# A mixer's state-space scan and gated network: context outputs and context network placed beneath the scan, one block of modulation products moved into the gated network, read-out tables and Toeplitz blocks in one array

## The chip, the cores and the metric

The kernel runs on one core of a Trainium2 chip. The metric is the device time of one execution in microseconds (us), the median of several runs. All times below are in microseconds unless they are marked otherwise.

## The reference, cut to what matters

The program is a small transformer block stack over 1024 latent positions and 256 context positions with 1024 channels (eight tiles of 128 channels each). The part that the change touches is the mixer of layer 0: a bidirectional state-space layer (S5), a pointwise GELU, a gated network, and a projection. Cut down, with names as in the program:

```
u   = modulate(norm(x)) @ w_s5_in                 # [1024 channels, 1024 latent + 256 context]
X_t = A X_{t-1} + B u_t                           # complex states, forward and backward, 64 groups
z   = gelu(C X + Toeplitz(P) u)                   # read-out tables times states, plus a local part
y   = (z @ w_s5_glu[u-half]) * sigmoid(z @ w_s5_glu[g-half])
x  += gate * (y @ w_s5_out)
mods[l, b] = silu(c) @ w_mod[l, b] + b_mod        # 24 blocks, two layers of 12, needed by later parts
```

Time is cut into chunks of 8 positions, so a state is stored for 128 latent chunks and 32 context chunks, and each of the 64 groups of 16 channels has three 128 by 128 blocks for the outputs: two read-out tables (real and imaginary part of C times powers of A) and one Toeplitz block (the part of the output within a chunk).

## The kernel before

The program is one long stream per engine: TensorE (PE) for products, VectorE (DVE) for the scan and the sums, ScalarE (ACT) for copies out of PSUM and activations, GpSimd (POOL) for a few products and stores, SyncE (SP) for nearly all loads. The order on each engine is fixed when the program is built; a wait of one instruction holds all that stand behind it on its engine. DMAs that SP or ACT issues share a small set of completion semaphores in rotation, so that a DMA also waits for one that was issued eight before it.

The parts around the change, in order of time:

- **Input projection** (0 to about 164): w_s5_in times the modulated input. DVE and POOL build tables beside it; read-out tables go to the DRAM array dT (`to`, L405), the Toeplitz part P goes to dPF (L436, L437), the projected input goes to dUL (latent) and dUC (context).
- **State input** (about 160 to 240): sixteen units, two for each block `fb` of eight groups. `s5_u_load` (L454 to L458) brings one block's input U into SBUF (one latent load, two copies of the context part), DVE builds the unit's table (L476), PE transposes it (L502), ACT copies it (`tin`, L504), PE multiplies (`s5_in`, L515, L516), and ACT writes the result into the state array X (L518). Units 0 to 7 fill X of the groups 0 to 31, units 8 to 15 that of the groups 32 to 63.
- **Scan** on DVE: `sa` over groups 0 to 31, `sb` over groups 32 to 63 (L537, L541, L543; three operations make one step). In its first 32 steps a scan carries latent and context states together (operations of double width), after that latent alone. Beneath it, PE runs the modulation products: 20 blocks here, each loaded by SP in eight pieces of 256 KB (`gw`, L164), multiplied (L174, columns of four quarters of the array at once), copied by ACT (L177), transposed (L184) and added to `mods` (L195, L196).
- **S5 outputs**, one block fb after the other: SP loads U again (L454, L455), the tables `tt` (L565 or L571) and the eight pieces of the Toeplitz block `G` (L574); ACT or DVE copies the states (`S`, L585 to L589); PE multiplies 24 products of 161 columns (L601, L603: 128 latent, one empty, 32 context); ACT applies GELU (L604); POOL stores dZL and dZC (L605, L606).
- **Gated network** on w_s5_glu: SP loads dZL back (16 loads) and dZC (8 loads), L1621; then, for each of the eight tiles, seven Winograd products of the latent part (`ffn_step`, L978, 12 records of 512 columns each for one half) and two products `G` and `U` of the context part (L988, 24 records of 256 columns each). Weights `wr` come by SP (L906), ACT and DVE round and sum them (L936, L940).
- Then the projection w_s5_out (L121 to L125), attention and the feed-forward networks, which the change leaves as they are.

Of the kernel before, what the change touches and what calls it, by code (L numbers as in the profile page):

```python
# [6 lines left out]
F32 = mybir.dt.float32  # L7
# [6 lines left out]
P = 128  # L14
# [14 lines left out]
class Kernel:  # L29
# [170 lines left out]

    def mod(self, l, w):

        return self.mods[:, l, 8 * w:8 * w + 8, :]
# [6 lines left out]
class S5(Kernel):  # L210
# [8 lines left out]
    def s5_load(self):  # L219
# [3 lines left out]
        self.CN = po.tile([P, NG, 2, 16], F32, name="CN")  # L223
# [6 lines left out]
    def s5_params(self):  # L230
# [126 lines left out]
        self.PO = self.prmo.tile([P, 3, 8, NG], F32, name="PO")  # L357
# [37 lines left out]
    def s5_out_table(self, u):  # L395
# [9 lines left out]
        nc.gpsimd.dma_start(self.dT[u // 2, :, 4 * (u % 2):4 * (u % 2) + 4], t[:, :, :, 1:9, :])  # L405
# [32 lines left out]


# [7 lines left out]
    def s5_u_load(self, pool, fb, both, bufs=3):  # L447
# [4 lines left out]
        uc = self.dUC[fb].rearrange("(p g) c -> p g c", g=8)  # L452
        nc.scalar.activation(U[:, :, 161:162], self.zero, AF.Copy)
        nc.sync.dma_start(U[:, :, 33:161], ul)  # L454
        nc.sync.dma_start(U[:, :, 162:194], uc)  # L455
        if both:
            nc.scalar.activation(U[:, :, 32:33], self.zero, AF.Copy)
            nc.sync.dma_start(U[:, :, 0:32], uc)  # L458
        return U

# [35 lines left out]
    def s5_in_trans(self, t):  # L496
        nc = self.nc
        tin = self.inpool.tile([P, 8, P], F32, tag="tin", bufs=3, name=self.nm("tin"))
# [59 lines left out]
    def s5_out_load(self, fb):  # L558
        nc = self.nc
        g0 = 8 * fb  # L560
        U = self.s5_u_load(self.upool, fb, False, 4)
        src = self.dT[fb].rearrange("p g r q c -> p g r (q c)")
        if fb % 4 < 2:
            t = self.upool.tile([P, 8, 2, 128], F32, tag="tt", bufs=2, name=self.nm("tt"))
            nc.sync.dma_start(t, src)  # L565
            tt = [t[:, 2 * i:2 * i + 2] for i in range(4)]
        else:

            tt = [self.gpool.tile([P, 2, 2, 128], F32, tag="gw", name=self.nm("tt")) for _ in range(4)]
            for i in range(4):  # L570
                nc.sync.dma_start(tt[i], src[:, 2 * i:2 * i + 2])  # L571
# [4 lines left out]
        return U, tt, G  # L576

    def s5_states(self, fb, vector):
# [4 lines left out]
        S = self.upool.tile([P, 8, 2, 161], F32, tag="S", bufs=2, name=self.nm("S"))  # L583
        if vector:
            nc.vector.tensor_copy(S[0:64], X[0:64, gs, :, 0:161])  # L585
        else:
            nc.scalar.activation(S[0:64], X[0:64, gs, :, 0:161], AF.Copy)
        nc.scalar.activation(S[64:128, :, :, 0:128], X[64:128, gs, :, 127::-1], AF.Copy)
        nc.scalar.activation(S[64:128, :, :, 128:161], X[64:128, gs, :, 161:128:-1], AF.Copy)  # L589
        return S  # L590

    def s5_out(self, fb, loaded, S):

        nc = self.nc
        U, tt, G = loaded
        Z = self.upool.tile([P, 8, 161], F32, tag="Z", bufs=2, name=self.nm("Z"))
        for a, n in ((0, 3), (3, 3), (6, 2)):
            ps = self.psum()
            for k in range(n):
                o = ps[:, 161 * k:161 * k + 161]  # L600
                nc.tensor.matmul(o, G[:, a + k, :], U[:, a + k, 33:194], start=True, stop=False)  # L601
                for ri in range(2):
                    nc.tensor.matmul(o, tt[(a + k) // 2][:, (a + k) % 2, ri, :], S[:, a + k, ri, :], start=False, stop=(ri == 1))  # L603
# [1480 lines left out]
```

## Time and profile before

| what | value |
|---|---|
| time, median of 3 runs | 3369.47 (3367.6 to 3373.42) |
| the profiled execution: its own time, and span of its instructions | 3376.47, 3372.8 |
| PE busy in the span | 3196.8 (95%) |
| DVE busy | 2057.7 (61%) |
| ACT busy | 1383.7 (41%) |
| POOL busy | 266.7 (8%) |
| data moved | 375.67 MB, mean 111 GB/s |

PE is the busiest engine over the whole span, but not in every stage: the shares are means over stages with different limits. The profiled execution is 7.0 us above the median of the timed runs. "PEclk" in the profile is the clock of TensorE that was granted, in shares of the full 2.4 GHz; a value between 0.5 and 1 in a window means that part of it ran at the lower level of 1.2 GHz.

### The profile page before, as it was taken

The page shows a single profiled execution, that of the slowest core. Times are in us where ns is not written, and L with a number is a line of the kernel's source. Part 1 is how long each engine was busy: PE and PEld are TensorE (multiplying, and loading weights), DVE is VectorE, ACT ScalarE, POOL GpSimd, SP SyncE. Part 2 cuts the span into 40 slices and gives each one's busy share as a digit, 9 for nine tenths or more (in the row PEclk, how much of TensorE's full clock was granted, in tenths as well). Part 3 has the DMA queues.
Part 4 walks back from the last instruction along what each step waited for, and adds up shares of the span by engine and source line. Part 5 has one row for each costly group of instructions (what it writes and reads, how often), then busy time and mean ns, then how long its engine had stood idle before and what let it go on. Part 6 is the DMA issues. An engine that isn't in the chain of part 4 may idle for free.

```text
span 3372.8 us, 47213 instructions
## 1 busy us (share of the span) xinstructions
PE 3196.8 (95%) x17814; PEld 2692.5 (80%) x17814; DVE 2057.7 (61%) x4313; ACT 1383.7 (41%) x2708; POOL 266.7 (8%) x286
## 2 busy tenths in 40 slices
PE   8999669998899999999999999999889999999997
PEld 5763558886788888888878899999778888888787
DVE  7789737545764444523666888886557445444645
ACT  3351434235432222412553577774453223233433
POOL 1230100010000000000012310001100000000000
PEclk9999879998899999999999999999989999999998
DMA  7679962241231122524521100002223221235534
GB/s 254 170 208 322 249 175 88 94 156 63 84 101 68 69 68 71 187 88 131 161 85 58 62 23 17 21 15 76 81 80 104 71 72 65 72 125 173 177 124 145
DMA packets 227668, 375.67 MB, mean 111 GB/s; under 512 B 54432, under 2 KB 111040, under 8 KB 226672
## 3 DMA queue, kind: packets, MB, share of 16 engines
q1 hardware_dynamic: 206416, 326.73, 30.5%
q0 software_dynamic: 7632, 25.35, 2.5%
q10 hardware_dynamic: 13392, 20.58, 1.7%
q8 instruction: 139, 2.28, 0.3%
q14 instruction: 89, 0.73, 0.1%
HBM read 291.84 MB, written 80.74 MB: 110 GB/s over the span
## 4 chain that ended last, share of the span: by engine, by line
PE 81%; DVE 12%; DMA 3%; ACT 2%; issue 1%; SPq 1%; ACTq 0%; POOL 0%; DVEq 0%; POOLq 0%
PE ps L978 28%; PE ps L121 10%; PE ps L123 10%; PE ps L125 10%; PE ps L988 8%; PE ps L1425 2%; DVE sw L537 1%; PE ps L1445 1%; PE ps L1446 1%; PE ps L1444 1%; PE ps L1383 1%; PE ps L1384 1%; PE ps L1385 1%; DVE X L543 1%; DVE sw L541 1%
## 5 line engine op out<-in xcount | busy, mean ns | idle before, releaser
L978 PE MATMUL ps<-pg,pg 128*128 128x512 f32 x4368 | 1035.8, 395 | 39.1 <-ACT pg L936 22.8
L978 PEld LDWEIGHTS ps<-pg,pg 128*128 128x128 f32 x4368 | 823.9, 191 | 217.0 <-ACT pg L936 24.6
L121 PE MATMUL ps<-pg,pg 128*128 128x512 f32 (+1 forms) x1872 | 635.2, 363 | 19.5 <-ACT pg L102 8.0
L125 PE MATMUL ps<-pg,pg 128*128 128x512 f32 (+1 forms) x1872 | 626.9, 358 | 4.8 <-DVE pg L103 4.8
L123 PE MATMUL ps<-pg,pg 128*128 128x512 f32 (+1 forms) x1872 | 629.7, 359 | 0.3
L121 PEld LDWEIGHTS ps<-pg,pg 128*128 128x128 f32 x1872 | 348.2, 191 | 81.4 <-ACT pg L102 9.7
L125 PEld LDWEIGHTS ps<-pg,pg 128*128 128x128 f32 x1872 | 348.2, 191 | 60.3 <-DVE pg L103 8.0
L123 PEld LDWEIGHTS ps<-pg,pg 128*128 128x128 f32 x1872 | 348.7, 191 | 55.1 <-DVE pg L132 1.7
L988 PEld LDWEIGHTS ps<-pg,pg 128*128 128x128 f32 x2496 | 320.9, 195 | 24.3 <-DVE pg L940 10.0
L988 PE MATMUL ps<-pg,pg 128*128 128x256 f32 x2496 | 326.3, 287 | 13.9 <-DVE pg L940 8.7
L103 DVE TENSOR_TENSOR pg<-wr,pg 128x512 fp32r<-128x512 f32 (+1 forms) x312 | 219.5, 733 | 189.5 <-ACT pg L102 115.2
L102 ACT ACTIVATE pg<-wr 128x512 fp32r<-128x512 f32 (+1 forms) x312 | 175.4, 596 | 271.2 <-DMA wr<-in_w_ffn_out 89.2
L940 DVE TENSOR_TENSOR pg<-pg,pg 128x512 fp32r<-128x512 f32 x208 | 142.5, 688 | 136.3 <-ACT pg L936 129.2
L940 DVE TENSOR_TENSOR pg<-wr,pg 128x512 fp32r<-128x512 f32 x232 | 158.1, 687 | 104.4 <-ACT pg L936 102.5
L936 ACT ACTIVATE pg<-pg 128x512 fp32r<-128x512 f32 x208 | 127.2, 628 | 154.5 <-DVE pg L931 59.0
L132 DVE TENSOR_TENSOR pg<-ps,pg 128x512 fp32r<-128x512 f32 (+1 forms) x210 | 141.9, 676 | 57.8 <-ACT pg L131 52.5
L936 ACT ACTIVATE pg<-wr 128x512 fp32r<-128x512 f32 x232 | 139.5, 624 | 79.6 <-PE ps L988 37.2
L1405 ACT ACTIVATE pg<-ps,nb,rq 128x512 f32<-128x512 f32 x192 | 148.9, 777 | 5.4 <-DVE sm L1414 2.4
L131 ACT ACTIVATE pg<-ps 128x512 fp32r<-128x512 f32 (+1 forms) x210 | 123.9, 591 | 64.1 <-PE ps L1425 47.6
L1155 POOL TENSOR_TENSOR pg<-pg,pg 128x512 f32<-128x512 f32 x8 | 10.7, 1332 | 1763.5 <-DVE pg L631 864.5
L631 DVE SCALAR_TENSOR_TENSOR pg<-ps,mods,pg 128x512 f32<-128x512 f32 x64 | 47.9, 749 | 165.4 <-PE ps L125 160.7
L1390 DVE TENSOR_REDUCE mx<-ps 128x1 f32<-128x512 f32 (+1 forms) x208 | 137.1, 661 | 1.3 <-PE ps L1385 1.3
(339 smaller groups left out, 4450.6 us busy)
## 6 DMA issues: line engine op xcount, KB each, us to landing
wr<-in_w_ffn_in SPq DMA_DIRECT2D x104, 512.0 KB, 3.5
gw<-in_w_mod SPq DMA_DIRECT2D x192, 256.0 KB, 5.2
wr<-in_w_ffn_out SPq DMA_DIRECT2D x80, 512.0 KB, 3.9
dI<-pg SPq DMA_DIRECT2D x104, 256.0 KB, 2.0
pg<-dI SPq DMA_DIRECT2D x104, 256.0 KB, 4.6
wr<-in_w_ffn_out SPq DMA_DIRECT2D x40, 384.0 KB, 4.0
dX<-pg ACTq DMA_DIRECT2D x48, 256.0 KB, 2.0
pg<-dX SPq DMA_DIRECT2D x48, 256.0 KB, 4.2
```

Of the source, the lines that this page charges most:

```text
L102: nc.scalar.activation(hi, x, AF.Copy)
L103: nc.vector.tensor_tensor(lo, x, hi.bitcast(F32), op=ALU.subtract)
L121: mm(ps[c], wh, rh[c], start=first, stop=False)
L123: mm(ps[c], wh, rl[c], start=False, stop=False)
L125: mm(ps[c], wl, rh[c], start=False, stop=last)
L132: self.nc.vector.tensor_tensor(lo, src, hi.bitcast(F32), op=ALU.subtract)
L936: nc.scalar.activation(hi, self.isum[i, name], AF.Copy)
L940: v.tensor_tensor(lo, self.isum[i, name], hi.bitcast(F32), op=ALU.subtract)
L978: mm(e[bank], p[:, o], q, start=(first and k == 0 and j == 0), stop=(k == 3 and j == 2), skip_group_check=True)
L988: mm(ps, p[:, o], q, start=(k == 0 and j == 0), stop=(k == KT - 1 and j == 2))
L1390: v.tensor_reduce(mx[:, kc:kc + 1], ps, axis=AX.X, op=ALU.max)
L1405: nc.scalar.activation(p, u["bank"].pop((qt, kc)), AF.Exp, bias=nb[:, 0:1], scale=rq, accum_out=sm[:, kc:kc + 1])
```

## The change

It has three parts.

1. **Layer 1's modulation** (12 of the 20 blocks that ran beneath the scan) becomes 48 quarter blocks in the gated network. `gemv_next` (new) multiplies one quarter that is there and loads the next but two, four loads of 128 KB each on ACT's DMA queue; after each fourth quarter come one copy and four transposes. It is called for each unit of the network's start from the third on, and once in each later step.
2. **The context's outputs and its whole gated network** become items of a list (`ctx_items`, new) that are run beneath the scan, at the places where the clock of the program's builder passes their time. They use PE (32 columns for the outputs, 256 for the network, without Winograd sums), ACT (copies, GELU, sigmoid) and POOL (stores, loads of dZC, products). The latent outputs shrink from 161 to 128 columns, the gated network that follows is started without a context part, and the eight dZC loads ahead of it are gone.
3. **Tables and Toeplitz blocks lie in one DRAM array dW**: the tables are stored into it by POOL in pieces of 512 B, the Toeplitz part is spread into it by eight DMAs from DRAM to DRAM (`s5_shifts`, 512 KB each) that SP issues when unit 5 starts, and an output block then needs one load of 1.5 MB instead of `tt` and eight pieces of `G`. The context input is loaded once into SBUF (`Uc`), and ACT copies it twice into each block's U (`s5_u_fill`, ahead of the copies of unit 2fb-1).

```diff
+    def gemv_next(self):
+        nc = self.nc
+        if len(self.gv) == 3 or not self.todo and self.gv:
+            l, b, z, t = self.gv.pop(0)
+            if z == 0:
+                self.gp = self.psum()
+            h, a = z // 2, z % 2
+            for q in range(4):
+                nc.tensor.matmul(self.gp[32 * q:32 * q + 32, 256 * h:256 * h + 256], self.sS[:, 4 * a + q, :], t[q],
+                                 start=(a == 0), stop=(a == 1), tile_position=(0, 32 * q), skip_group_check=True)
+            if z == 3:
+                s = self.page()
+                nc.scalar.activation(s, self.gp, AF.Copy)
+                self.gemv_fin(l, b, self.gemv_tr(s))
+        if self.todo:
+            l, b, z = self.todo.pop(0)
+            t = [self.half() for _ in range(4)]
+            for q in range(4):
+                nc.scalar.dma_start(t[q], self.I["w_mod"][l, b, :, 4 * (z % 2) + q, 256 * (z // 2):256 * (z // 2) + 256])
+            self.gv.append((l, b, z, t))
...
+    def s5_shifts(self):
+        src = self.dPF.rearrange("g c t h -> c g (t h)")
+        for i in range(8):
+            self.nc.sync.dma_start(self.dW[16 * i:16 * i + 16].rearrange("p f g r c -> p (f g) r c")[:, :, 2],
+                              src[:, :, 16 * (7 - i):16 * (7 - i) + 128])
...
+    def s5_u_fill(self, fb, U):
+        for o in (32, 161):
+            self.nc.scalar.activation(U[:, :, o:o + 1], self.zero, AF.Copy)
+        for o in (0, 162):
+            self.nc.scalar.activation(U[:, :, o:o + 32], self.Uc[:, 8 * fb:8 * fb + 8, :], AF.Copy)
...
-        G = self.upool.tile([P, 8, 128], F32, tag="G", bufs=4, name=self.nm("G"))
-        for i in range(8):
-            nc.sync.dma_start(G[16 * i:16 * i + 16],
-                              self.dPF[g0:g0 + 8].rearrange("g c t h -> c g (t h)")[:, :, 16 * (7 - i):16 * (7 - i) + 128])
...
+    def ctx_items(self):
...
+        def out(fb, h):
+            U, t = ld[fb]
...
+            for k in range(4 * h, 4 * h + 4):
+                o = ps[:, 32 * k:32 * k + 32]
+                nc.tensor.matmul(o, t[:, k, 2, :], U[k], start=True, stop=False)
+                for ri in range(2):
+                    nc.tensor.matmul(o, t[:, k, ri, :], sc[fb][:, k, ri, :], start=False, stop=(ri == 1))
...
+        def net(t, h, ks=range(KT)):
...
+            for k in ks:
+                nc.tensor.matmul(ps, W[2 * t + h][:, P * k:P * k + P], self.zc[:, k, :], start=(k == 0), stop=(k == KT - 1))
...
+                nc.gpsimd.tensor_tensor(u, u, sc["g"], op=ALU.mult)
+                nc.gpsimd.dma_start(self.dI[t][:, 1024:1280], u)
...
         self.x_start(zz)
-        for c in (0, 1, 2):
+        for c in (0, 1):
             zload(c)
...
+                for _ in range(GN if k > GK else 0):
+                    self.gemv_next()
...
         def one(u):
+            if u == 0:
+                self.s5_u_fill(0, U[0])
+            if u % 2 and u < 15:
+                self.s5_u_fill(u // 2 + 1, U[u // 2 + 1])
             self.nin += 1
+            if self.nin == 6:
+                self.s5_shifts()
             self.s5_in(u, tin.pop(u), U[u // 2])
             if u % 2 and u // 2 + 2 < 8:
-                U.append(self.s5_u_load(self.inpool, u // 2 + 2, True, 2))
+                U.append(self.s5_u_load(self.inpool, u // 2 + 2, 2))
```

**SP's queue at the state input.** These are the issues on SP before, from the input of block 2 (U_1865) to that of block 5 (U_2162):

```order
L454 DMA U_1865<-dUL 128x8x128
L455 DMA U_1865<-dUC 128x8x32
L458 DMA U_1865<-dUC 128x8x32
L454 DMA U_1967<-dUL 128x8x128
L455 DMA U_1967<-dUC 128x8x32
L458 DMA U_1967<-dUC 128x8x32
L454 DMA U_2071<-dUL 128x8x128
L455 DMA U_2071<-dUC 128x8x32
L458 DMA U_2071<-dUC 128x8x32
L454 DMA U_2162<-dUL 128x8x128
```

And now, over the same four blocks (U_2103 is block 4):

```order
L484 DMA Uc<-dUC 128x256
L485 DMA U_1887<-dUL 128x8x128
L484 DMA Uc<-dUC 128x256
L485 DMA U_1990<-dUL 128x8x128
L467 DMA dW<-dPF 1024x1x128 x8
L484 DMA Uc<-dUC 128x256
L485 DMA U_2103<-dUL 128x8x128
L484 DMA Uc<-dUC 128x256
L485 DMA U_2195<-dUL 128x8x128
```

The eight copies from DRAM to DRAM stand between the loads of block 3 and block 4.

**ACT's queue at units 6 and 7.** Before, the tables (`tin`) and the copies into X (X_1697 is the array of groups 0 to 31) follow each other; these are the last rows of unit 6 and the first of unit 7:

```order
L518 ACTIVATE X_1697<-ps_2113 128x2x161
L518 ACTIVATE X_1697<-ps_2119 128x2x161
L504 ACTIVATE tin_2125<-ps_2126 128x512
L504 ACTIVATE tin_2125<-ps_2132 128x512
L518 ACTIVATE X_1697<-ps_2138 128x2x161
```

Now, at the same place (the array is X_1711):

```order
L551 ACTIVATE X_1711<-ps_2142 128x2x161
L551 ACTIVATE X_1711<-ps_2148 128x2x161
L537 ACTIVATE tin_2154<-ps_2155 128x512
L537 ACTIVATE tin_2154<-ps_2161 128x512
L490 ACTIVATE U_2103<-zero 128x8 x2
L492 ACTIVATE U_2103<-Uc 128x8x32 x2
L551 ACTIVATE X_1711<-ps_2171 128x2x161
```

The fill of block 4's U, which waits for that block's load, stands ahead of unit 7's copies into X.

**PE in the gated network.** Before, a context product `U` (L988) stands between the latent products of two tiles:

```order
L988 MATMUL ps_5212<-pg_5193,pg_5099 128x256 x2
L988 MATMUL ps_5212<-pg_5193,pg_5107 128x256
L978 MATMUL ps_5109<-pg_5067,pg_5105 128x512
L978 MATMUL ps_5109<-pg_5065,pg_5139 128x512
L978 MATMUL ps_5109<-pg_5089,pg_5105 128x512
```

Now, in the network's start, quarter blocks (L210; `hp` are the half pages into which ACT's queue loads w_mod) and transposes (L184) stand between the products (L1100):

```order
L1100 MATMUL ps_5074<-pg_4733,pg_4936 128x512
L210 MATMUL ps_4962<-hp_4967,sS 32x256
L210 MATMUL ps_4962<-hp_4968,sS 32x256
L210 MATMUL ps_4962<-hp_4969,sS 32x256
L210 MATMUL ps_4962<-hp_4970,sS 32x256
L1100 MATMUL ps_4987<-pg_4737,pg_4851 128x512
```

The context products are gone from there, and each step has four short products of another shape.

## Rows read from the trace of the kernel before

**Rows 1.** Windows: PE, PEld, DVE, ACT, POOL busy (count), PEclk, DMA share, GB/s.
```profile
250.00:300.00 50.00, 48.23 (x190) 15.48 (x188) 49.79 (x202) 5.32 (x16) 2.16 (x8) 0.99 0.95 320
...
450.00:500.00 50.00, 27.70 (x100) 21.25 (x101) 23.10 (x37) 20.47 (x35) 1.73 (x2) 0.76 0.64 167
...
600.00:680.00 80.00, 80.00 (x428) 69.37 (x428) 38.70 (x65) 24.82 (x47) 0.00 (x0) 1.00 0.27 93
```

**Rows 2.** Timeline of SP: start, duration, queue, line, transfer.
```profile
180.33 1.18 SPq L454 DMA_DIRECT2D U<-dUL  x1
...
189.56 0.52 SPq L454 DMA_DIRECT2D U<-dUL  x1
```

**Rows 3.** Timeline of ACT, then DVE, at the scan's start.
```profile
195.34 2.08 ACT L518 ACTIVATE X<-ps 128x322 f32<-128x322 f32 x4
...
197.52 0.73 DVE L537 TENSOR_TENSOR sw<-X,sm 128x256 f32<-128x256 f32 x1 [1.94 <-ACT X L518]
```

**Rows 4.** DMA issues: count, KB each, median us to landing.
```profile
U<-dUL SPq DMA_DIRECT2D x16, 512.0 KB, 5.0
```

**Rows 5.** Chain that ended last, 400 to 500: start, us, what.
```profile
405.09 9.24 DMA G<-dPF
...
449.47 0.45 ACT Z L604
...
450.52 5.93 DMA dZL<-Z
...
463.34 0.83 SPq L1621
...
471.27 4.46 DMA wr<-in_w_s_glu
```

**Rows 6.** Timeline of DVE: the first step that is single-width in both scans.
```profile
301.08 0.26 DVE L541 TENSOR_TENSOR sw<-sw,X 128x64 f32<-128x64 f32 x1
```

**Rows 7.** Timeline of PE: modulation blocks, then outputs.
```profile
264.25 1.05 PE L184 MATMUL ps<-sel,gs 128*128 128x2 f32 x8
...
270.48 1.05 PE L184 MATMUL ps<-sel,gs 128*128 128x2 f32 x8
...
371.02 1.41 PE L603 MATMUL ps<-S,tt 128*128 128x161 f32 x4 [11.45 <-DVE S L585]
...
376.36 0.43 PE L601 MATMUL ps<-U,G 128*128 128x161 f32 x2
...
377.18 0.43 PE L601 MATMUL ps<-U,G 128*128 128x161 f32 x2
```

**Rows 8.** Line L184: counts, durations in ns, first and last start.
```profile
L184 PE MATMUL ps<-sel,gs x192: 169/251/353, 13.0 to 351.2; 128*128 128x2 f32 x192
```

**Rows 9.** Timeline of PE: context product, half a modulation block; PEld: weight loads of one.
```profile
557.68 3.04 PE L988 MATMUL ps<-pg,pg 128*128 128x256 f32 x24
560.55 5.63 PE L978 MATMUL ps<-pg,pg 128*128 128x512 f32 x24
...
14.01 1.06 PE L174 MATMUL ps<-gw,sS 128*32 128x512 f32 x8
...
265.24 0.23 PEld L174 LDWEIGHTS ps<-gw,sS 128*32 128x32 f32 x4
```

**Rows 10.** Timeline of DVE and POOL at 700; POOL's groups by line.
```profile
700.12 4.01 DVE L103 TENSOR_TENSOR pg<-wr,pg 128x512 fp32r<-128x512 f32 x4
699.96 1.28 POOL L1155 TENSOR_TENSOR pg<-pg,pg 128x512 f32<-128x512 f32 x1 [247.71 <-DMA wr<-in_w_s_out]
701.19 1.20 POOL L1155 TENSOR_TENSOR hp<-hp,hp 128x256 f32<-128x256 f32 x1
...
L1157 POOL TENSOR_TENSOR hp<-hp,hp 128x256 f32<-128x256 f32 x20 | 18.4, 920 | 43.4 <-DVE hp L631 43.4
```

**Rows 11.** DVE's costliest group of that shape on its own.
```profile
L940 DVE TENSOR_TENSOR pg<-pg,pg 128x512 fp32r<-128x512 f32 x208 | 142.5, 688 | 136.3 <-ACT pg L936 129.2
```

**Rows 12.** Line L1582, issues on ACT's queue: ns minimum, median, maximum.
```profile
L1582 ACTq DMA_DIRECT2D dX<-pg x48: 326/326/849, 780.9 to 2499.9; - x48
```

More of the change, by code (lines that the diff above doesn't have):

```diff
@@ L594, in s5_out @@
         nc = self.nc
-        U, tt, G = loaded
-        Z = self.upool.tile([P, 8, 161], F32, tag="Z", bufs=2, name=self.nm("Z"))
-        for a, n in ((0, 3), (3, 3), (6, 2)):
+        U, t = loaded
+        Z = self.upool.tile([P, 8, 128], F32, tag="Z", bufs=2, name=self.nm("Z"))
+        for a in (0, 4):
             ps = self.psum()
-            for k in range(n):
-                o = ps[:, 161 * k:161 * k + 161]
-                nc.tensor.matmul(o, G[:, a + k, :], U[:, a + k, 33:194], start=True, stop=False)
+            for k in range(a, a + 4):
+                o = ps[:, 128 * (k - a):128 * (k - a) + 128]
+                nc.tensor.matmul(o, t[:, k, 2, :], U[k], start=True, stop=False)
@@ L602, in s5_out @@
                 for ri in range(2):
[L603 to L606 removed]
+                    nc.tensor.matmul(o, t[:, k, ri, :], S[:, k, ri, :], start=False, stop=(ri == 1))
@@ L886, in x_rest, with i_start @@
         self.x_flush()
-    def i_start(self, win, pairs, first):
+    def i_start(self, win, pairs, first, ctx=True):
         self.win = win
@@ L1063, in ffn_body @@
                     self.x_all(*{"P6": ("T3",), "P5": ("T4",), "P7": ("B22",)}.get(kind, ()))
+                for _ in range(GN):
+                    self.gemv_next()
         self.X = self.hs = self.xr = self.xt = self.ev = None
@@ L1889, in mixer0 @@
         todo = [(0, b) for b in range(4, 12)] + [(1, b) for b in range(12)]
+        NGV = len(todo) - GL
         g, sm, tp = [self.gemv_load(*todo[0])], {}, {}
         gk = [0]
+        self.todo, self.gv = [(l, b, z) for l, b in todo[NGV:] for z in range(4)], []
         def gemv_step():
@@ L1940, in mixer0, with counted @@
         self.prm.release()
+        self.upool = tc.alloc_tile_pool(name="uo", bufs=2, side="left", reuse_waits="tile")
+        def counted(gen):
+            for k, t in enumerate(gen):
+                if k == 3 * 33:
+                    items.append(self.ctx_items())
+                yield t
+        sb = counted(sb)
+        self.ld = []
         drive(sa, sb, 1)
-        while gk[0] < 20:
+        while gk[0] < NGV + 2:
             gemv_step()
-        self.upool = tc.alloc_tile_pool(name="uo", bufs=2, side="left", reuse_waits="tile")
-        ld = [self.s5_out_load(i) for i in range(4)]
         self.dense = False
@@ L1975, in mixer0 @@
             clock(10)
-        while gk[0] < 22:
-            gemv_step()
+        for it in items:
+            for _, f in it:
+                f()
         self.upool.release()
+        self.prmo.release()
         self.gpool.release()
```

193 lines of the change are left out of this document (132 added, 61 removed).

## The prediction

> **What bounds the kernel now.** I read the busy time by windows first. While the scan runs, DVE has no gap (49.79 of 50 us between 250 and 300); at the end of the output stage no engine is full (PE 27.70 of 50 between 450 and 500, its granted clock 0.76); in the gated network PE is full (80.00 of 80) [rows 1]. So the stretch has three limits, and a part of the change is worth what it does to the limit of its own stage. Then the chain of waits, for the stage in which nothing is full: it goes through loads of Toeplitz pieces (9.24 us for the block that starts at 405), the last GELU at 449.47, the store of dZL (5.93), the sixteen loads of dZL, the eight of dZC (463.34 to 471.27), and the weight load behind them in SP's queue (4.46) [rows 5]. Last the timelines where the scan starts: its first operation, at 197.52, waits 1.94 us for ACT's copies of unit 7 into X, which ran from 195.34 [rows 3].
>
> **The network's start.** The eight dZC issues are gone from the chain: 471.27 - 463.34 = -7.9 [rows 5]. The dZL loads keep their number and sizes.
>
> **The end of the outputs.** Before, a block is six records in 0.82 us for each of eight groups (376.36 to 377.18) [rows 7], 6.6 us at the full clock, but each of the last four waits for Toeplitz pieces. At 128 columns the product is 0.82 x 128/161 = 0.65, so 5.2 a block and 42 for eight, and one load three blocks ahead takes the place of nine, so PE should no longer wait there. In exchange the context work must be done beneath the scan or between the outputs. Its products: outputs with 48 records a block; records with almost no columns still take 1.05 us for eight [rows 7], so 6.3 a block, 50 in all; the network 16 x 8 products of 256 columns at 0.27 x 256/161 = 0.44, so 3.5 each and 56 in all. Room: twenty modulation blocks become eight at 6.2 us pace (264.25 to 270.48) [rows 7]; the last ended at 351.2 [rows 8], so now near 351 - 12 x 6.2 = 276. Blocks 4 to 7 can start when sb leaves its context steps, at 301 [rows 6], and end near 329; with a store and a load (12 us) between, the networks start near 341. By 372, when the latent outputs can start (before, the first waited for the states until 371.0 [rows 7]), some 31 us of the 56 are through, and 25 + 42 + about 7 for waits in ACT's order put the last output near 446 against 450 before: -3. Bounds: -8 if PE never waits, 0 if ACT's order costs 4 more. With the start, **-11**.
>
> **The scan's start.** This is where something is added. SP issues the eight copies to dW directly behind block 3's input (180.33) and ahead of block 4's (189.56) [rows 2], and on ACT the fill of block 4 now stands ahead of unit 7's copies, for which the scan waits. A late block 4 thus delays the scan one for one, though the scan's first steps don't need it. How long 4.19 MB take from DRAM to DRAM no row shows. Nearest in size of piece (512 B) is the window with the dZL loads, 167 GB/s at a share of 0.64 [rows 1], 261 GB/s when full: 16 us. Fast end: 320 GB/s at 0.95 [rows 1], 13. Slow end: reading and writing each take that time, 32. From 182 (two issues of block 3 stand behind 180.33), the copies end at 195, 198 or 214. Block 4's 640 KB behind them (2.5 us, or 5 at half speed) and some 1 us of latency land near 198, 201.5 or 220. If nothing held them they would land at 189.56 + 5.0 [rows 4] = 194.6. From landing to the scan: fill, four short copies, about 1.2, then 2.1 for unit 7 [rows 3], so the scan starts at 201.5, 205, 223, or 198 with no delay. Against 197.52 that is +4, **+7**, +26, or 0. I take +7, by the row with the same piece size. Cover to lose there is none: DVE has no gap behind it.
>
> By the Trainium skill, "DMA: Bandwidth & Descriptors", section "Queues, rings and completion order", descriptors of one queue on one engine are consumed in ring order, so block 4's input cannot overtake the copies. That speaks against the change; no row of this trace has a small load behind a large copy on SP. By that rule the 0 end falls away and the sum stands.
>
> **DVE beside POOL.** The context network puts eight POOL products of 256 columns (0.92 each) [rows 10] into this stretch, some five of them beneath the scan. What they cost DVE: four DVE operations took 4.01 us beside 2.48 us of POOL [rows 10], against 4 x 0.688 = 2.75 for the same shape [rows 11]: 1.26, half of POOL's time. So 5 x 0.92 x 0.5 = 2.3; twelve short sums of `mods` leave the scan and give back about 1. **+1**, between -1 and +4.
>
> By the Trainium skill, "SBUF — State Buffer", section "Who interferes with whom", a DVE operation with two SBUF inputs and a GpSimd one that reads SBUF exclude each other for the whole instruction. By it the five would cost up to 4.6 and the sum 2 more; the row shows half.
>
> **The gated network.** PE is full there, so PE's sum decides. Gone: 16 context products at 560.55 - 557.68 = 2.87 [rows 9]: -45.9. Added: 48 quarter blocks; half a block before (8 records of 512 columns) took 1.06 [rows 9], and a quarter now has the same 8 records with half the columns. If the columns set the pace a quarter is 0.5 (24 in all), if the records do, 1.06 (51). I take 0.5: of what belongs to a record the 32-wide weight load is the long part, and four of those took 0.23 [rows 9], so eight fit into 0.5. Transposes: 12 x 1.05 [rows 7] = 12.6. Sum -9.3. Then ACT issues 192 loads at 0.33 (0.85 at most) [rows 12], 63 us into a stretch where it is busy 24.82 of 80 [rows 1]: room, but in order ahead of copies that PE waits for, so I add 4 (0 to 12). The rounding of the context's inputs goes: -2. **-8**, from -13 to +10; with records at 1.06 it would be +19.
>
> **Sum.** -11 + 7 + 1 - 8 = -11. The profiled execution takes 3376.5, so 3365.5; it lies 7.0 above the median of the runs, and on the median 3369.5 the same -11 gives **3358.5**. About 0.2% (6.7 us) is what a measurement of this kernel can tell from no change.
>
> **Rivals.**
> 1. *The copies are slow, slower overall.* They run at half the nearest rate; the scan starts 26 later. Then -11 + 26 + 1 - 8 = +8: 3377. It decides when the scan starts later than 215, from which the total is above zero (block 4 then lands after 212). For it: each piece is both read and written in DRAM. Against: the one window with such pieces gives 261 when full [rows 1]. 0.15.
> 2. *The copies cost nothing.* Block 4 lands as before: -18: 3351. For it: the copies are issued some 8 us before block 4 was. Against: the pieces of 512 B, and that a single queue carries both. 0.17.
> 3. *The quarter blocks make the gated network wait*: a step can't go on because ACT sits in a DMA issue that waits for a half page, or records set the pace. Body +10 instead of -8: total +7, 3376. For it: ACT is in order and 32 of the issues fall into the start, where ACT is most used. Against: ACT has over half of its time free, DMA share is 0.27 [rows 1]. 0.14.
> 4. *The context work doesn't fit*: the last output ends at 460 rather than 446, total +3: 3372. For it: the stage is then PE's. Against: the room counted above, and DMA, nearly full beneath the scan (a share of 0.95 [rows 1]), gets no more to do: 25 MB of modulation leave, and about as much (tables for the context's outputs, the network's weights) comes. 0.04.
>
> **How the numbers follow.** My forecast has 0.50: copies that cost 3 to 12, a body between -13 and -2, so 3349 to 3367. Of it about 0.39 is faster by over 0.2%, 0.11 within. Rival 2: all 0.17 faster. Rival 1: 0.07 within, 0.08 slower. Rival 3: 0.05 within, 0.09 slower. Rival 4: 0.03 within, 0.01 slower. Sum: faster 0.56, same 0.26, slower 0.18. The two slow rivals could also fall together, so I move 0.03 from same to slower. The range for 8 in 10 takes the good case (-27: a body of -13 and outputs of -8) and most of the two slow ones (+13): 3342 to 3382.
>
> **What would show it.** The copies: DVE's first scan operation near 205, idle before it about 9 and put down to ACT, and ACT's fill (U from Uc) waiting for a DMA; at 198 rival 2, at 223 rival 1. The outputs: PE nearly full from 372 to the last output, no idle put down to Toeplitz pieces, the granted clock near 1 rather than 0.76; the last GELU near 454 (446 plus the delay). The start: from the last GELU to the first long row of products about 19 rather than 27. The body: mean pitch of a quarter block near 0.5, PE full; idle before products put down to ACT or to `hp` would be rival 3. DVE: scan operations that lengthen beside POOL's products by about half their time. The forecast is wrong in sign if the scan starts later than 215 or if the network's body is longer than before by over 3 us.

## The result, and the profile after

The changed kernel takes 3412.62 (median of 4 runs, 3407.41 to 3415.06), the kernel before 3369.14 (4 runs): a ratio of 1.0125, 95% interval 1.0107 to 1.0142. It is slower by 43, where 3358.5 and a gain were forecast. The profiled execution has a span of 3410.2 against 3372.8, so 37.4 are to be found in the trace.

**Windows of the changed kernel**, columns as in [rows 1].

```profile
250.00:300.00 50.00, 46.50 (x205) 30.57 (x205) 49.45 (x193) 10.05 (x21) 3.08 (x9) 0.77 0.76 275
300.00:350.00 50.00, 50.00 (x237) 50.00 (x236) 50.00 (x274) 7.21 (x14) 6.63 (x9) 0.50 0.60 212
400.00:450.00 50.00, 46.38 (x308) 43.26 (x307) 11.62 (x44) 29.86 (x29) 7.21 (x12) 0.97 0.83 293
450.00:500.00 50.00, 30.48 (x213) 28.56 (x212) 8.72 (x12) 16.40 (x24) 3.46 (x6) 0.81 0.78 241
```

Between 300 and 350 TensorE has no idle time, yet the granted clock is 0.50, the lower level of 1.2 GHz. [Rows 1] had 0.99 beneath the scan from 250 to 300. Here two engines are full at once, DVE with the scan and PE with the context's outputs. The clock was 1.00 from 265 to 274, while the last modulation products ran, and 0.50 from 278 to 280, when the context's outputs had begun (277.67, behind a wait of 1.48 for their table).

**PE's timeline of the changed kernel**: two groups of context outputs, the first network products, the first latent outputs, the first long row of the gated network, three steps of that network, and its end.

```profile
285.34 0.61 PE L665 MATMUL ps<-Uc,tt 128*128 128x32 f32 x2
285.77 1.04 PE L667 MATMUL ps<-scx,tt 128*128 128x32 f32 x4
286.62 0.61 PE L665 MATMUL ps<-Uc,tt 128*128 128x32 f32 x2
...
359.58 9.04 PE L698 MATMUL ps<-zc,wr 128*128 128x256 f32 x26
...
402.06 0.38 PE L629 MATMUL ps<-ul,tt 128*128 128x128 f32 x2
...
500.31 13.60 PE L1100 MATMUL ps<-pg,pg 128*128 128x512 f32 x48 [3.65 <-ACT pg L1058]
...
704.59 0.64 PE L210 MATMUL ps<-hp,sS 128*32 128x256 f32 x8
705.16 3.02 PE L1100 MATMUL ps<-pg,pg 128*128 128x512 f32 x12
708.11 0.64 PE L210 MATMUL ps<-hp,sS 128*32 128x256 f32 x8
...
712.20 2.12 PE L1100 MATMUL ps<-pg,pg 128*128 128x512 f32 x8
714.16 0.95 PE L184 MATMUL ps<-sel,pg 128*128 128x2 f32 x8
714.97 1.17 PE L1100 MATMUL ps<-pg,pg 128*128 128x512 f32 x4
716.20 0.50 PE L121 MATMUL ps<-pg,pg 128*128 128x512 f32 x1
...
717.84 5.61 PE L1100 MATMUL ps<-pg,pg 128*128 128x512 f32 x24
723.29 0.39 PE L125 MATMUL ps<-pg,pg 128*128 128x512 f32 x1
```

A group of six records starts every 286.62 - 285.34 = 1.28, a block of eight groups takes 10.24, and the context's networks begin at 359.58 (forecast 341), the latent outputs at 402.06 (forecast 372). In the gated network a step of 12 products and a quarter block takes 708.11 - 704.59 = 3.52. The last 24 products of the network now stand behind the projection's first ones; alone they take 723.29 - 717.84 = 5.45, so 12 take 2.73 and the quarter block beside them 0.79. The last 12, with four transposes among them, take 716.20 - 712.20 = 4.00: 1.27 for the transposes.

**ACT, then DVE, of the changed kernel** at the scan's start and ahead of the gated network.

```profile
206.59 0.73 ACT L492 ACTIVATE U<-Uc 128x256 f32<-128x256 f32 x2 [5.58 <-DMA Uc<-dUC]
...
476.17 0.60 ACT L632 ACTIVATE Z<-ps 128x512 f32<-128x512 f32 x1 [1.76 <-PE ps L631]
476.25 9.88 ACTq L220 DMA_DIRECT2D hp<-in_w_mod  x12
486.17 3.23 ACT L953 ACTIVATE pg<-pg 128x512 fp32r<-128x512 f32 x6 [9.41 <-DMA hp<-in_w_mod]
...
162.59 0.69 DVE L509 TENSOR_TENSOR ti<-tm,ps 128x512 f32<-128x512 f32 x1 [8.24 <-DMA Uc<-dUC]
...
208.73 0.49 DVE L570 TENSOR_TENSOR sw<-X,sm 128x256 f32<-128x256 f32 x1 [7.67 <-ACT X L551]
```

**The chain of the changed kernel** from the last GELU to the first long row: start, us, what.

```profile
476.25 4.39 DMA hp<-in_w_mod
...
480.70 5.08 DMA pg<-dZL
...
485.85 4.35 DMA pg<-dZL
...
493.66 5.88 DMA wr<-in_w_s_glu
...
499.62 0.64 ACT pg L1058
```

ACT's copies stand behind twelve issues (9.88), but they are not what ends last. SP's dZL loads wait for a w_mod load that ACT's queue had issued, and the weight load, for which ACT then waits 6.84, is issued only behind them. The dZL loads go to other buffers than the w_mod loads, so I take the shared completion semaphores for what ties them; no run shows that by itself.

Where the 37.4 are, stage by stage:

| stage | before | after | difference | forecast |
|---|---|---|---|---|
| last GELU of the outputs starts | 449.47 | 476.17 | +26.7 | +5 (454) |
| from there to the first long row of products | 27.0 | 24.1 | -2.9 | -7.9 |
| from there to the projection | 205.7 | 221.5 | +15.8 | -8 |
| the rest of the program (by difference) | | | -2.2 | 0 |

The third line starts at 476.51 before and 500.31 after and ends with the projection's first product (682.21 and 716.20); for versions of the change the 24 later products are added as 5.6. Below, this is "the network's stretch".

### The profile page after: what moved, and what is told of

Read it like the earlier page. It is cut to its first block, busy times and chain, and to the rows that moved or that the text cites. A ratio compares the mean times of both kernels' runs of the same rounds, so it can differ in the third digit from the quotient of the medians.

```text
span 3410.2 us, 48179 instructions
## 1 busy us (share of the span) xinstructions
PE 3254.1 (95%) x18262; PEld 2759.6 (81%) x18262; DVE 2036.1 (60%) x4279; ACT 1390.3 (41%) x2714; POOL 287.6 (8%) x326
## 4 chain that ended last, share of the span: by engine, by line
PE 76%; DVE 5%; ACT 3%; DMA 2%; issue 1%; ACTq 0%; SPq 0%; POOL 0%; DVEq 0%; POOLq 0%
PE ps L1100 29%; PE ps L121 9%; PE ps L123 8%; PE ps L125 8%; PE ps L1110 7%; PE ps L1549 2%; PE ps L1570 1%; PE ps L1569 1%; PE ps L1568 1%; PE ps L1507 1%; PE ps L1508 1%; PE ps L1509 1%; PE ps L829 1%; PE ps L210 1%; DVE pg L814 1%
## 5 line engine op out<-in xcount | busy, mean ns | idle before, releaser
L1100 PE MATMUL ps<-pg,pg 128*128 128x512 f32 x4368 | 1053.6, 399 | 35.3 <-ACT pg L1058 20.7
L1100 PEld LDWEIGHTS ps<-pg,pg 128*128 128x128 f32 x4368 | 826.1, 192 | 228.5 <-ACT pg L1058 22.1
L121 PEld LDWEIGHTS ps<-pg,pg 128*128 128x128 f32 x1872 | 347.2, 191 | 80.7 <-ACT pg L102 9.4
L125 PEld LDWEIGHTS ps<-pg,pg 128*128 128x128 f32 x1872 | 346.8, 190 | 60.8 <-DVE pg L103 8.5
L123 PEld LDWEIGHTS ps<-pg,pg 128*128 128x128 f32 x1872 | 347.5, 191 | 55.0 <-DVE pg L132 1.5
L103 DVE TENSOR_TENSOR pg<-wr,pg 128x512 fp32r<-128x512 f32 (+1 forms) x312 | 218.5, 729 | 196.2 <-ACT pg L102 123.6
L1110 PEld LDWEIGHTS ps<-pg,pg 128*128 128x128 f32 x2112 | 271.7, 196 | 21.5 <-DVE pg L1062 8.5
L1110 PE MATMUL ps<-pg,pg 128*128 128x256 f32 x2112 | 276.7, 288 | 12.4 <-DVE pg L1062 7.2
L1062 DVE TENSOR_TENSOR pg<-wr,pg 128x512 fp32r<-128x512 f32 x214 | 145.7, 686 | 92.9 <-ACT pg L1058 92.2
L1058 ACT ACTIVATE pg<-wr 128x512 fp32r<-128x512 f32 x214 | 128.7, 624 | 74.5 <-PE ps L1110 33.6
```

The source lines that it names most:

```text
L103: nc.vector.tensor_tensor(lo, x, hi.bitcast(F32), op=ALU.subtract)
L121: mm(ps[c], wh, rh[c], start=first, stop=False)
L123: mm(ps[c], wh, rl[c], start=False, stop=False)
L125: mm(ps[c], wl, rh[c], start=False, stop=last)
L1058: nc.scalar.activation(hi, self.isum[i, name], AF.Copy)
L1062: v.tensor_tensor(lo, self.isum[i, name], hi.bitcast(F32), op=ALU.subtract)
```

## The experiments

Two theories stood after the result. One: TensorE is late with the context's outputs, because their products of 32 columns leave it at the lower clock; the scan's later start is hidden behind that. The rival: the late scan start (208.73 for 197.52) and what waits for it delay the outputs. For the second loss, the network's stretch, the question was whether the quarter blocks themselves or waits around them cost it. Stages are read from one profiled execution of each version. The network's stretch with all 48 quarter blocks is 221.5 in the changed kernel, 220.4 in shift16, 218.5 in wide2, 216.5 in wide4 and 214.6 in w4_pool, although the network's code is the same; differences of a few us there say little. Where a version had a single run, its time is given, but nothing rests on it.

**wide4: the context's output products stream their 32 columns four times.** The result is read from the first copy; TensorE does four times the columns. The results of four groups have a PSUM tile of their own, and GELU is applied in halves.

```diff
+            R = 4
...
+            wide = lambda x: x[:, None, :].to_broadcast([P, R, 32])
...
-                o = ps[:, 32 * k:32 * k + 32]
-                nc.tensor.matmul(o, t[:, k, 2, :], U[k], start=True, stop=False)
+                o = ps[:, k - 4 * h]
+                nc.tensor.matmul(o, t[:, k, 2, :], wide(U[k]), start=True, stop=False)
...
```

> The changed kernel, but each product of the context's outputs streams its 32 columns four times over (128 columns, a repeat in the access pattern; the result is the same). Theory A (the context's outputs are slow because TensorE is granted only 1.2 GHz while it streams 32 columns per weight load): the clock between 280 and 350 goes from 0.50 to near 1.00 and a block of 48 records from 10.24 us to about 5.4, what the latent blocks of 128 columns take at 402. The first four blocks end near 300, the last four wait for the scan (about 312) and end near 335, so the network beneath the scan starts some 25 earlier and the total falls by about 25, to near 3388. Rival B (it is the amount of weight loads and traffic beneath the scan, whatever the columns): the clock stays at 0.50, a block takes 10.24 or more, the total stays at 3412 or rises. Rival C (the late start of the scan, 208.7 against 197.5, is what is carried to the end): the total stays within 3 of 3412.

Measured: 3391.15 (4 runs), ratio to before 1.0053 (1.0037 to 1.0070). PE's timeline of wide4: a group at the lower clock, one at the higher, the wait behind them, and the first product of the context's networks:

```profile
279.76 0.64 PE L666 MATMUL ps<-Uc,tt 128*128 128x128 f32 x2
280.19 1.06 PE L668 MATMUL ps<-scx,tt 128*128 128x128 f32 x4
281.04 0.63 PE L666 MATMUL ps<-Uc,tt 128*128 128x128 f32 x2
...
286.04 0.39 PE L666 MATMUL ps<-Uc,tt 128*128 128x128 f32 x2
286.26 0.61 PE L668 MATMUL ps<-scx,tt 128*128 128x128 f32 x4
286.71 0.39 PE L666 MATMUL ps<-Uc,tt 128*128 128x128 f32 x2
...
308.33 1.22 PE L668 MATMUL ps<-scx,tt 128*128 128x128 f32 x4 [6.49 <-ACT scx L647]
...
332.25 1.03 PE L699 MATMUL ps<-zc,wr 128*128 128x256 f32 x4
```

Windows of wide4 beneath these products:

```profile
280.00:300.00 20.00, 20.00 (x167) 20.00 (x167) 20.00 (x84) 4.99 (x11) 3.53 (x5) 0.92 0.84 314
280.00:284.00 4.00, 4.00 (x24) 4.00 (x24) 4.00 (x18) 1.01 (x2) 0.00 (x0) 0.61 0.95 402
290.00:300.00 10.00, 10.00 (x92) 10.00 (x91) 10.00 (x42) 2.13 (x5) 2.92 (x4) 1.00 0.93 339
```

The first products run at the lower clock here too, behind a wait for their table (0.61 on average from 280 to 284), and a group of 128 columns then takes 281.04 - 279.76 = 1.28, as one of 32 does in the changed kernel. But here the clock rises, and at 1.00 a group takes 286.71 - 286.04 = 0.67. TensorE now waits for context states, which ACT copies out of the scan (6.49). The networks start at 332.25 for 359.58 and the last GELU at 452.11 for 476.17; the forecast had 341 and 454. Four times the columns in half the time: this loss is the clock, shown.

**wide2: the same with 64 columns** (`R = 2`).

> As the run with four repeats, with two (64 columns). Theory A, if 64 columns are enough for the full clock: a block near 6.3 (48 records at the pace of records with few columns), total about 20 below 3412. If 64 columns are not enough: clock 0.50, a block 10.2 to 11, total as the changed kernel. Rival B: as the changed kernel in any case.

Measured: 3406.71 (one run), last GELU at 476.07, as in the changed kernel. The window of wide2:

```profile
320.00:340.00 20.00, 20.00 (x95) 20.00 (x95) 20.00 (x115) 3.70 (x8) 2.91 (x4) 0.50 0.60 211
```

The clock stays at 0.50 and the count of records in 20 us is 95, as with 32 columns (96 between 300 and 320 there). The run also rules out the other edits of wide4 (GELU in halves, another PSUM layout) as the cause of its gain.

**shift16: the eight copies to dW are issued behind the last input load.**

```diff
-            if self.nin == 6:
+            if self.nin == 16:
                 self.s5_shifts()
```

> The changed kernel, but the eight copies from DRAM to DRAM are issued after the last block's input load instead of between those of block 3 and block 4. Both theories: DVE's first scan operation comes some 5 earlier (204 instead of 208.7), because ACT's fill of block 4 no longer waits 5.58 for its load. Rival C (the scan's start is carried to the end): total -5, 3407. Theory A (TensorE's queue of context work sets the end of the outputs): total within 2 of the changed kernel.

Measured: 3409.48 (4 runs), ratio 1.0104 (1.0089 to 1.0120). DVE's timeline of shift16:

```profile
203.66 0.49 DVE L570 TENSOR_TENSOR sw<-X,sm 128x256 f32<-128x256 f32 x1 [1.98 <-ACT X L551]
```

The scan starts 5.1 earlier, and the last GELU only 2.1 (474.05). So the copies cost the scan's start 5.1, and less than half of that reaches the last GELU: the rival is out as the main cause.

**nomod: the 48 quarter blocks and their loads are left out.** Layer 1's modulation is set to zero, so that part of the result is left out.

```diff
-        self.todo, self.gv = [(l, b, z) for l, b in todo[NGV:] for z in range(4)], []
+        nc.gpsimd.memset(self.mods[:, 1], 0.0)
+        self.todo, self.gv = [], []
```

> The changed kernel without layer 1's modulation products: they are neither loaded nor multiplied, the modulation of layer 1 is set to zero (that part of the result is left out). It measures what the quarter blocks cost in the gated network. By the prediction's term (0.5 a quarter, 1.05 a transposed block, 4 of waits) the stretch from the first long row of products to the projection falls by about 41. By the reading of the trace after (0.79 a quarter, since a switch between products costs, 1.27 a transposed block, some waits) by about 56. The start, from the last GELU to the first long row, falls by some 5, since ACT issues no twelve loads there (9.88 us of its queue).

PE's timeline of nomod:

```profile
496.99 20.08 PE L1100 MATMUL ps<-pg,pg 128*128 128x512 f32 x74 [3.84 <-ACT pg L1058]
...
539.08 6.09 PE L1100 MATMUL ps<-pg,pg 128*128 128x512 f32 x15 [4.91 <-DVE pg L1134]
...
656.59 0.50 PE L121 MATMUL ps<-pg,pg 128*128 128x512 f32 x1
```

The time is 3357.88 (one run). The stretch is 656.59 - 496.99 + 5.6 = 165.2 (165.7 in w4_gl0 below, which has no quarter blocks either). So the quarter blocks with all that belongs to them cost 221.5 - 165.2 = 56.3 in the changed kernel, and 49 in w4_pool, the lowest (forecast 24 + 12.6 + 4 = 40.6). Without them 205.7 - 45.9 - 2 = 157.8 was forecast, so 7.4 are missing there too. From the last GELU (477.34) to the long row it is 19.65, as forecast (19), for 24.1 in the changed kernel: the w_mod loads took the rest.

**tables_only: the third part alone on the kernel before**, copies issued behind the last input load, context loads as before.

```diff
+        t = self.upool.tile([P, 8, 3, 128], F32, tag="tt", bufs=3, name=self.nm("tt"))
+        nc.sync.dma_start(t, self.dW[:, fb])
+        return U, t
...
+            if self.nin == 16:
+                self.s5_shifts()
```

> The kernel before with the third part of the change alone: tables and Toeplitz blocks in one array, one load of 1.5 MB for each output block, three blocks ahead; the copies from DRAM to DRAM are issued after the last block's input load, so the scan starts as before (197.5). Theory A says that of the change only the context work and the quarter blocks cost time, so this part alone gains what the waits for Toeplitz pieces cost: the last four blocks follow each other at 6.6 to 7.5 us, the last GELU near 433 instead of 449.5, total -10 to -18, near 3357. Rival (the copies cost as much as they save, since they run among the modulation loads beneath the scan): the modulation ends after 371, the first output block starts later by as much, total within 5 of before.

Measured: 3356.19 (4 runs), ratio 0.9956 (0.9939 to 0.9973): faster than both kernels. Two output blocks on PE's timeline of tables_only, then its last GELU on ACT's:

```profile
400.31 0.51 PE L598 MATMUL ps<-U,tt 128*128 128x161 f32 x2 [0.31 <-DMA tt<-dW]
...
427.66 0.51 PE L598 MATMUL ps<-U,tt 128*128 128x161 f32 x2 [0.36 <-DMA tt<-dW]
...
434.52 0.44 ACT L601 ACTIVATE Z<-ps 128x322 f32<-128x322 f32 x1 [1.07 <-PE ps L600]
```

Where the chain of [rows 5] held a load of 9.24, these two output blocks wait 0.31 and 0.36 for their table, and no other block waits for its own; the last GELU comes at 434.52 for 449.47.

**tables_early: tables_only with the copies where the change has them** (`self.nin == 6`).

> The run with the third part alone, but the eight copies are issued where the change has them, between the input loads of block 3 and block 4. There the scan is what the outputs wait for, so the prediction's step (a late block 4 delays the scan one for one and the end with it) can be seen by itself: the copies took about 16 in the changed kernel, so block 4 lands near 203 instead of 195, the scan starts 6 to 9 later (205 to 208) and the total is 5 to 8 above the run with the copies later (3356): near 3363. In this version ACT does not copy the input, so only TensorE's unit 8 waits for block 4, and units 0 to 7, on which the scan's first half rests, do not: by that the scan's start moves by 2 at most and the total stays within 3 of 3356. I hold the second for likelier (0.7).

Measured: 3362.05 (10 runs, 3356.36 to 3368.22), ratio 0.9975 (0.9962 to 0.9987). SP's timeline of tables_early, then DVE's:

```profile
182.47 12.65 SPq L446 DMA_DIRECT2D dW<-dPF  x8
...
196.01 1.01 DVE L546 TENSOR_TENSOR sw<-X,sm 128x256 f32<-128x256 f32 x1 [1.94 <-ACT X L527]
```

Same copies, same place in SP's queue, no later scan. In the changed kernel it is both together: copies ahead of block 4's input, and ACT's fill, which waits for that input, ahead of the copies that the scan waits for. The total missed the expectation: it is 6 above that of tables_only, where at most 3 were expected with the scan unmoved. The two versions were timed against different runs of the kernel before and the intervals of their ratios overlap; what the 6 are, if they are real, stays open.

**w4_pairs: wide4, quarter blocks two at a time in every second step.** If the 0.29 above the 0.5 belongs to the change from one shape to another, half of the changes go.

```diff
...
-                for _ in range(GN if k > GK else 0):
+                self.gk += k > GK
+                for _ in range(2 * (self.gk % 2) if k > GK else 0):
                     self.gemv_next()
...
```

> The run with four repeats, with the quarter blocks done two at a time at every second step instead of one at each. If what a quarter costs above 0.5 is the switch between the two kinds of product (some 0.29 each time), 24 switches are gone: the stretch from the first long row of products to the projection falls by 7, span near 3374. If it is the quarter itself, nothing changes (3381); if the eight loads in a row on ACT's queue hold ACT's copies, the stretch grows.

Measured: 3390.08 (one run). The stretch is 211.5 + 5.6, against 210.9 + 5.6 in wide4: no gain of 7 that could be seen. PE's timeline of w4_pairs:

```profile
518.45 1.07 PE L210 MATMUL ps<-hp,sS 128*32 128x256 f32 x16
```

Two quarters in a row take some 1.0 to the next product (519.45), so a pair is cheaper in itself than 2 x 0.79, but idle time came in at the transposes, and the granted clock from 550 to 600 is 0.93, where wide4 has 1.00. Whether the 0.29 belongs to the change of shape stays open: one profile of each can't tell it in a stretch that varies by 7.

**w4_pool: wide4, the w_mod loads on GpSimd's queue instead of ACT's.**

```diff
-                nc.scalar.dma_start(t[q], self.I["w_mod"][l, b, :, 4 * (z % 2) + q, 256 * (z // 2):256 * (z // 2) + 256])
+                nc.gpsimd.dma_start(t[q], self.I["w_mod"][l, b, :, 4 * (z % 2) + q, 256 * (z // 2):256 * (z // 2) + 256])
```

> The run with four repeats, with the loads of the quarter blocks issued on GpSimd's queue instead of ACT's. If ACT's queue is what costs the start (its first twelve issues stand 9.88 us ahead of the copies there), the time from the last GELU to the first long row falls from 22 to near 18, and the gaps of the start that are put down to ACT shrink: span 3381 less 4 to 6. If the loads cost by their traffic, the start stays as it is. If GpSimd's issues hold VectorE, the stretch of the network grows.

Measured: 3387.57 (one run). ACT's timeline of w4_pool:

```profile
473.18 1.15 ACT L1059 ACTIVATE pg<-wr 128x512 fp32r<-128x512 f32 x2 [9.10 <-DMA wr<-in_w_s_glu]
```

The start is 473.86 - 453.22 = 20.6, against 474.49 - 452.11 = 22.4 in wide4: 1.8 of the 4 expected. The weight load ends last here as in the changed kernel, but the chain behind the last GELU now goes through the store of dZL (4.71) instead of a w_mod load, as it does in nomod (5.45).

**w4_gl0, w4_gl5, w4_c10: how many of layer 1's blocks to move** (wide4 with late copies; `GL` 0, 5 and, with pairs, 10 instead of 12).

> Four repeats, copies issued late, and no block moved into the gated network: all twenty blocks stay beneath the scan together with the context's work (the second and third part without the first). The network from its first long row to the projection falls to about 160, as in the run without layer 1's products (56 less than in the changed kernel). Beneath the scan the twelve blocks come back at 6 each, paced by their loads; if the context's products fit into TensorE's waits for these loads, the last GELU moves from 452 to about 475 and the total is near 3358; if they only queue up behind them, to about 505 and the total is near 3388. Theory A says nothing between the two; the loads beneath the scan (40 MB of modulation, 24 of tables, 8 of weights) at 300 GB/s need 240 of the 250 there are, so I expect nearer the second, 3380.

> As the run before it with five blocks moved into the gated network instead of none. Each block costs 4 x 0.79 + 1.27 = 4.4 in the network and 6 beneath the scan where DMA paces it. If loads beneath the scan bind, this is about 5 x (6 - 4.4) = 8 below the run with none; if TensorE's waits there take the blocks for nothing, it is up to 20 above.

> All together: four repeats, copies issued after the last input load, quarter blocks in pairs, and ten instead of twelve blocks moved into the gated network (two more stay beneath the scan). By the reading so far, against the run with four repeats: copies -3 (the scan starts 5 earlier, and with the full clock the last four context blocks wait for the scan), pairs -6, two blocks fewer in the network -9, two more beneath the scan +3: some -15, so a total of 3376 and a span near 3366, 6 below the span before. If TensorE's room beneath the scan is used up, two blocks more there cost 12 and the sum is near zero.

| version | moved | median (runs) | ratio to before | last GELU | first long row | projection |
|---|---|---|---|---|---|---|
| wide4 | 12 | 3391.15 (4) | 1.0053 (1.0037 to 1.0070) | 452.11 | 474.49 | 685.34 |
| w4_gl0 | 0 | 3416.97 (4) | 1.0139 (1.0119 to 1.0160) | 499.01 | 558.8 | 718.87 |
| w4_gl5 | 5 | 3395.96 (1) | | 472.85 | 518.41 | 697.27 |
| w4_c10 | 10 | 3379.35 (10) | 1.0025 (1.0016 to 1.0035) | 449.94 | 472.42 | 677.41 |

PE's timeline of w4_gl0, products of the context's network behind the last latent outputs:

```profile
506.19 5.38 PE L699 MATMUL ps<-zc,wr 128*128 128x256 f32 x16 [3.76 <-DMA wr<-in_w_s_glu]
```

With no block moved the stretch falls to 718.87 - 558.8 + 5.6 = 165.7, as in nomod, but the last GELU comes 47 later than in wide4 and the long row some 60 after it: beneath the scan there is no room for the modulation and the context's work together. Six of the context network's sixteen groups of products are left behind the outputs, and five of them wait 3.5 to 3.9 for their weights. The expectation missed that: it had 3380, and 3388 at worst. With ten blocks 3376 was expected and 3379.35 measured. None of these settings brings the change below the kernel before. The first part without the second was not run.

**tables_zc: tables_only, and the eight dZC loads go behind the network's first weight loads.** This tries the term of -7.9 on its own.

```diff
-        for c in (0, 1, 2):
+        for c in (0, 1):
             zload(c)
...
+                if k == 1:
+                    zload(2)
```

> The run with the third part alone (copies issued late), and the eight loads of dZC moved behind the first three weight loads in SP's queue. It tests the prediction's term for the network's start by itself, without the context work: the eight issues stood 8.3 us ahead of the weight load that the first long row waits for. If they are what is waited for, the time from the last GELU to the first long row falls from 24.8 to near 17, and the total from 3356 to near 3348. If the weight load then waits for something else (the sixteen dZL loads, traffic), less than half of that is seen.

Measured: 3355.47 (4 runs), ratio 0.9952 (0.9935 to 0.9968). From the last GELU (431.88) to the long row of tables_zc, on PE's timeline:

```profile
449.86 18.71 PE L975 MATMUL ps<-pg,pg 128*128 128x512 f32 x74 [3.62 <-ACT pg L933]
```

18.0, against 459.27 - 434.52 = 24.8 in tables_only: -6.8, and the stretch behind it is 208.7 for 207.6. The timed medians (3355.47, 3356.19) don't tell the two apart, where 8 less was expected: the term is seen in its stage, in one pair of profiles, and not in the total. With tables_only it is the fastest version run, and it beats both kernels.

## Why the prediction was wrong

Two terms failed, with misses of about the same size: the end of the outputs (22 of the 48 by which the profiled difference, +37.4, lies off the forecast's -11) and the gated network (24). The start adds 5, and the rest of the program gives back 2.

- **"The end of the outputs": the first step that failed.** Context outputs were priced at 6.3 a block, 50 in all, by a row at the full clock [rows 7]. They took 10.24 and 82. The row itself was near (wide4, at the higher clock, 5.36 a block); what failed is that the clock was carried over from another kind of work. The networks began 18.6 behind the forecast's 341, the latent outputs at 402.06, and from there the forecast's 446 - 372 = 74 held (476.17 - 402.06 = 74.1), so the last GELU is 22 behind the 454. The forecast's sign for this term, "the granted clock near 1", was set for the time from 372 on. It came true there (0.97 from 400 to 450) and could not deny anything: the time had been lost before.
- **"The gated network": the second step, a sum mis-sized in two terms.** -8 was forecast and +15.8 measured (+8.9 in w4_pool, the lowest profile). The forecast named "longer than before by over 3 us" as a sign of being wrong. A quarter block costs 0.79 in a steady step, not 0.5 (halfway to the 1.06 of the other bound, [rows 9]), and four transposes 1.27, not 1.05: 48 x 0.79 + 12 x 1.27 = 53.2 of nomod's 56.3. Idle time ahead of products behind the first long row is 10.4 in the changed kernel and 7.4 in nomod, which about makes up the rest. The other 7.4 are what nomod's stretch has above the forecast's 157.8. Its idle times sum to 7.4 (1.29, 0.29, 0.38, 0.20, 0.32, 4.91), those of before to 5.9 (1.00, 0.27, 0.36, 0.22, 0.37, 3.35, 0.33): 1.5. Between 540 and 600 nomod's granted clock is 0.96 where before has 1.00 (520 to 580): 60 x 0.04 = 2.4. Ahead of that, nomod has 0.86 (497 to 520) and 0.94 (520 to 540) where before has 0.93 and 1.00: at most another 23 x 0.07 + 20 x 0.06 = 2.8. So the removed context products had not been worth their full 45.9.
- **"The network's start": right in mechanism, mis-sized.** nomod (19.65) and tables_zc (-6.8, in the stage alone) show the -7.9 nearly whole. The change keeps 2.9 of it, since SP's dZL loads, and with them the weight load, wait behind the w_mod loads. The prediction had ACT's issues hold ACT's copies and put 4 for it into the gated network; that a load on ACT's queue would hold loads on SP's was in no term.
- **"The scan's start": right in the delay, not in its price.** +7 was forecast for the copies and shift16 measured 5.1. Another 6.1 were not foreseen. The trace has an idle time of 8.24 ahead of DVE's table operation at 162.59, put down to a load of `Uc` on which its inputs don't depend; I take it for a place in SBUF that is used again, and that was not tried. The sum carried the delay one for one to the end; of shift16's 5.1, 2.1 reached the last GELU, since the scan wasn't what ended last. How the copies held the load is also not as it was summed: SP took 12.54 to issue the eight (188.25 to 200.79), and the load behind them landed some 5.7 after its own issue at 200.83, against a median of 5.2 for the loads of `Uc`. By the Trainium skill, "DMA: Bandwidth & Descriptors", section "Queues, rings and completion order", descriptors of one queue are consumed in ring order on each engine, though a later one may finish its write before an earlier one. No run here shows that order at work; the 1 us of latency in the prediction's sum is in no row either.
- **"DVE beside POOL": nothing to see.** The scan ran 200.8 (208.73 to 409.5) against 204.1 (197.52 to 401.6).
- **The rivals.** The third (quarter blocks, body +10, at 0.14) and the fourth (the context work doesn't fit, outputs 14 later, at 0.04) both came about, and both larger than priced: a body of +15.8 and a last GELU 22 later. The third's mechanism is only half there: a quarter's pace lies between its two bounds, and little of it is idle time. For the fourth only products were counted into the room, never the clock they would run at. That the two slow rivals (the copies and the quarter blocks) fall together had been given 0.03; the pair that fell together was another.
- **The third part** was right: Toeplitz waits were on the chain, and without them the kernel gains 0.44% alone.

## What to carry to other kernels

A duration per instruction holds only at the clock at which its row was taken: when work of another shape moves into a stage, look for a row where that shape ran alone and for a long time, and read the granted clock beside it. A change made of several parts is worth running in parts: the third alone was faster than before, and the rest of the change hid it. Work that moves into a stage whose engine is already full costs its whole time there, and what leaves that stage gives back less than its own time where the engine then waits or runs at a lower clock.

## What the runs showed of the hardware

- TensorE, busy without a gap, stayed at 1.2 GHz from 300 to 350 with products of 32 or 64 columns per 128 by 128 weights (95 or 96 records in 20 us either way). With 128 columns the granted clock was 0.61 from 280 to 284 and 1.00 from 290 to 300, and a group of six records took 1.28 and 0.67. Streaming the same columns four times made the kernel faster by 21 (3412.6 to 3391.2). What the granted clock goes by is not told by these runs.
- Eight copies of 512 KB from DRAM to DRAM in pieces of 512 B held a small load behind them on the queue until 206.6, 18 after the first was issued (188.25): 12.5 for issuing the eight and some 5.7 for the load. The prediction's sum had 19.5 for the same (182 to 201.5).
